# A bank of 512 columns for one token tile: new traversal of the output products in the merge blocks, and joint evictions of token-major pairs, in an encoder layer on one core

## The chip, the cores and the metric

The kernel runs on one core of a Trainium2 chip. The core has TensorE (PE in the profile; its weight loads are listed apart as PEld), VectorE (DVE), ScalarE (ACT), GpSimd (POOL) and SyncE (SP), which here issues nearly all DMAs. The metric is the device time of one execution in microseconds.

## The reference

Two sequences, `x_prompt` of 1024 tokens and `x_sample` of 2048, each with 16 meta tokens ahead of it, go through one encoder layer with shared weights and a model width of 1024. What is computed, cut to what matters here:

```python
xn = _rmsnorm(h, g_pre)
proj = xn @ w_in + b_in.astype(xn.dtype)
na_q, na_k, na_v, na_z, ml_qk, ml_v, ml_z, ml_o, ml_g, mg = jnp.split(proj, SPLIT_IDX, axis=-1)
ya = _neighbourhood_attention(...)
ya = (ya.reshape(B, L, NA_WIDTH) * jax.nn.silu(na_z)) @ w_a
yb = (_mlstm_branch(...) * jax.nn.silu(ml_z)) @ w_b
ga, gb = jnp.split(jax.nn.sigmoid(mg), 2, axis=-1)
y = (ga * ya + gb * yb) @ w_out
return h + _rmsnorm(y, g_post)
```

The change touches two places: the products with `w_out` (with the sum of squares that the last norm needs and the factor `g_post`), and the columns of the first projection that are kept token-major (`na_v`, `ml_v`, `ml_z`, `ml_o` and the gates).

## The kernel before

Everything is fp32 in memory. Each large product is made of three matmuls on parts of the operands that are split into a high and a low half (`whi`, `wlo` for weights; `xh`, `xl` or `mh`, `mlo` for data): high by high, high by low, low by high. TensorE's program order is the order in which the Python program emits it; for ACT, DVE, POOL and SP the compile step orders the instructions itself, by a simulated timeline, except for those that `self.behind` pins in program order. Two generators feed TensorE in turn: `dense` (projections and merges) and `sparse` (mLSTM and neighbourhood attention), each yielding an estimated PE time, so that the products of one are strewn among those of the other.

**Weights** come in units of 128 partitions by 1024 fp32. A unit lies in one of four pairs of buffers (`NBW = 4`, tiles `whi` and `wlo`). `wtake` hands out the next unit; `wdone` says that a unit has been used up, and `wpump` then fills the free pair with the next unit of a fixed list. A unit that is used for the first time is loaded raw (`wraw`, two buffers, line 245), split by ACT (line 271) and DVE (line 272) and written back in two parts (line 287). From its second use on it is loaded as two finished parts of 512 KB (line 264).

**PSUM banks** of 128 by 512 fp32 are named by tag: three for `pj` (projections, merges and output products), two for `tr`, one for `sc`, two for `sm`. The attention uses `tr`, `sc` and `sm` alone.

**Token-major projection**, `tm_unit`: for two weight units (halves of the contraction) and pairs of token tiles, each tile of a pair takes a `pj` bank of its own, 24 matmuls fill 256 (or 264) columns of it (lines 644 to 646), and DVE adds the bias into half `a` of a staging tile `stT` (line 661 for the second sequence, line 659 with a factor for the first). After the second tile `tm_store` sends the pair to memory.

**A merge block**, `final`, handles 512 tokens; there are six of them, two of `x_prompt` and four of `x_sample`. In its first half, the merge, eight column tiles by two branches are multiplied (lines 172 to 174 with `yh`, `yl`, 512 columns each) and gated by DVE (lines 2009 and 2011), and split into `mh` (ACT, 2012) and `mlo` (DVE, 2013). In its second half come the output products: `prods` issues 12 matmuls of 256 columns (lines 2042 to 2044) for one token tile, one weight unit (half of the contraction) and a quarter of the columns. For each quarter `cq` there are two banks, each with a pair of token tiles side by side, and two units; each unit is taken, used for the four token tiles and given back at once. After the second unit `leave` is called for both tiles of a bank: ACT squares 256 columns and sums them into one column of `ssq` (line 2047), then DVE multiplies the same 256 columns by `gpost` into `yo` (line 2048). So a full block has 32 calls of `prods`, eight units and 16 leaves. The last block has this order for two quarters only and then a tail in which the token tiles finish one after the other and go through `final_out` at once.

While the products run, a `hook` prepares the next block: `yload` loads its operands (`yl`, line 1936) and splits them with ACT (line 1956) and DVE (line 1940), one step for each call of `prods`. It starts after the sixth call. The attention's own loads (`qr`, `kr`, `gt`, `zt`, `vr`, lines 1310 to 1334), the gates `tg` (line 1981), residuals `xres` (2103) and stores (`out`, 2125) pass through the same SP queue as the weights.

Of the kernel before, what the change touches and what calls it, by code (L numbers as in the profile page):

```python
# [10 lines left out]
F32 = mybir.dt.float32  # L11
F32R = mybir.dt.float32r
I32 = mybir.dt.int32
AF = mybir.ActivationFunctionType
ALU = mybir.AluOpType
# [3 lines left out]
P = 128  # L19
TCARGS = dict(schedule_with_timeline_sim=True)  # L20
D = 1024
KT = D // P
# [95 lines left out]
def _bc(ap, off, n, parts=P):  # L118

    return bass.AP(tensor=ap.tensor, offset=ap.offset + off, ap=[[0, parts], [1, n]])  # L120

NBW = 4
C512, C256 = 0.235, 0.12
# [3 lines left out]
class K:  # L127
# [491 lines left out]
    def tm_unit(self, col, halves, wd):  # L619
        nc, wp = self.nc, self.wp  # L620
        ws = self.wtake(2)
        bb = wp.tile([P, WU], F32, name="bb", bufs=2)
        nc.sync.dma_start(bb[:, :wd], _bc(self.i["b_in"], col, wd))
        todo = []
        for x, s, t0, meta in halves:
            base = NM if meta else 0
            todo += [(x, s, base + 2 * P * j, P, 2, t0 + 2 * P * j) for j in range(2)]
            if meta and not (C_MZ <= col < C_GA - wd):
                todo.append((x, s, 0, NM, 1, None))
        for j, (x, s, c, n, cnt, tok) in enumerate(todo):  # L630
            st = wp.tile([P, 2, WU], F32, name="stT", bufs=4)
            for a in range(cnt):
                p = self.psum("pj", [P, 512])
                o = p[:n, :wd]
                xs = slice(c + a * P, c + a * P + n)
                for k in range(KT):
                    wh, wl = ws[k // 4][0][:, k % 4, :], ws[k // 4][1][:, k % 4, :]
                    if tok is None:
                        both = [(p[:48, :wd], self.xmm[:, k, :], wh), (o, self.xmm[:, k, :NM], wl)]
                        for y, (out, lhs, rhs) in enumerate(both if k < KT - 1 else both[::-1]):  # L640
                            nc.tensor.matmul(out, lhs, rhs, start=k == y == 0, stop=k == KT - 1 and y == 1, skip_group_check=True)
                    else:
                        xh, xl = x[0][:, k, xs], x[1][:, k, xs]
                        nc.tensor.matmul(o, xh, wh, start=k == 0, stop=False)  # L644
                        nc.tensor.matmul(o, xh, wl, start=False, stop=False)  # L645
                        nc.tensor.matmul(o, xl, wh, start=False, stop=k == KT - 1)  # L646
                    if k == 3:
                        if j == len(todo) - 1 and a == cnt - 1:
                            self.wdone()
                        yield (8 if tok is None else 12) * C256  # L650
                if j == len(todo) - 1 and a == cnt - 1:
                    self.wdone()
                if tok is None:
                    nc.scalar.activation(st[:n, 1, :wd], p[32:48, :wd], AF.Copy)
                    nc.vector.tensor_tensor(st[:n, 0, :wd], p[:n, :wd], st[:n, 1, :wd], op=ALU.add)
                    nc.vector.scalar_tensor_tensor(st[:n, 0, :wd], st[:n, 0, :wd], self.rc[:n, 8:9], bb[:n, :wd], op0=ALU.mult, op1=ALU.add)
                elif s == 0:
                    r = tok // P + a
                    nc.vector.scalar_tensor_tensor(st[:n, a, :wd], p[:n, :wd], self.rc[:n, r:r + 1], bb[:n, :wd], op0=ALU.mult, op1=ALU.add)
                else:  # L660
                    nc.vector.tensor_tensor(st[:n, a, :wd], p[:n, :wd], bb[:n, :wd], op=ALU.add)
                if a == cnt - 1:
                    self.tm_store(col, wd, s, n, cnt, tok, st)
                yield 12 * C256
# [1300 lines left out]
    def final(self, s, b, nxt):  # L1965
        nc, fp, i = self.nc, self.wp, self.i
        n, t0 = 512, 512 * b
# [3 lines left out]
        _, yh, yl = self.y  # L1971
# [18 lines left out]
        for ft, br in order:  # L1990
            if br:
                held[ft] = self.wtake(1)[0], tgs.pop(ft)
            w, ms = held[ft]
# [6 lines left out]
            p = self.psum("pj", [P, 512])  # L2000
# [18 lines left out]
            for _ in self.fout:  # L2019
                pass  # L2020
        yt = [fp.tile([P, D], F32, name="yo", tag="xr", bufs=4) for _ in range(4)]
        ssq = fp.tile([P, 4, 4], F32, name="ssq", bufs=2)
        sqj = fp.tile([P, 256], mybir.dt.bfloat16, name="sqj", tag="thT", bufs=1)
        hook = None
        if self.fresh:
            self.fresh = False
# [11 lines left out]
        def prods(o, tt, w, a, fresh):  # L2038
            xs = slice(tt * P, tt * P + P)
            for k in range(4):  # L2040
                f, q = 4 * a + k, w[0][:, k, :]
                nc.tensor.matmul(o, mh[:, f, xs], q, start=fresh and f == 0, stop=False, skip_group_check=True)  # L2042
                nc.tensor.matmul(o, mh[:, f, xs], w[1][:, k, :], start=False, stop=False, skip_group_check=True)  # L2043
                nc.tensor.matmul(o, ml[:, f, xs], q, start=False, stop=f == KT - 1, skip_group_check=True)  # L2044

        def leave(o, tt, cq):
            nc.scalar.activation(sqj, o, AF.Square, accum_out=ssq[:, tt, cq:cq + 1])
            nc.vector.tensor_tensor(yt[tt][:, cq * 256:(cq + 1) * 256], o, self.gpost[:, cq * 256:(cq + 1) * 256], op=ALU.mult)

        for cq in range(4 if nxt else 2):  # L2050
            banks = [self.psum("pj", [P, 2, 256]) for _ in range(2)]
            for a in range(2):
                w = self.wtake(1)[0]
                for tt in range(4):
                    prods(banks[tt // 2][:, tt % 2], tt, w, a, tt % 2 == 0)
                    if tt == 3:
                        self.wdone()
                    if a and tt % 2:
                        for t in (tt - 1, tt):
                            leave(banks[t // 2][:, t % 2], t, cq)  # L2060
                        if nxt and hook is None:
                            if nxt[0] != "f":
                                nres = []
                                hook = self.build_half(*nxt[:2], nres)
                            else:
                                hook = self.ystart(*nxt[1:])
                    if hook:
                        next(hook, None)
                    yield 12 * C256
        if not nxt:  # L2070
            ws = [[self.wtake(1)[0] for _ in range(2)] for _ in range(2)]
            for tt, cq in [(0, 2), (1, 2), (0, 3), (1, 3), (2, 2), (2, 3), (3, 2), (3, 3)]:
                o = self.psum("pj", [P, 512])[:, :256]
                for a in range(2):
                    prods(o, tt, ws[cq - 2][a], a, True)
                    if a == 0:
                        yield 12 * C256
                leave(o, tt, cq)
                if cq == 3:
                    for _ in self.final_out(s, t0, yt, ssq, tt, tt + 1):  # L2080
                        pass
                yield 12 * C256
            self.wdone(4)
# [183 lines left out]
```

## Time and profile before

| What | us |
|---|---|
| median of 3 runs | 2720.48 (2719.08 to 2722.17) |
| profiled execution, its own time | 2718.74 |
| its span | 2717.0 |
| PE busy in it | 2686.7 |
| DVE busy / ACT busy | 1766.1 / 1520.2 |
| first output product, last output product | begin at 2056.1 and 2708.4 |

The span is the time from the first instruction of the program to the last in the profiled execution. The 1.74 us between its span and its own time are outside any instruction. PE is busy in nearly the whole span; matmuls overlap in the pipeline (a matmul of 256 columns is listed at 0.28 us and the next one starts 0.12 us later), so counts of matmuls and stretches of time tell more than summed durations. The DMA traffic is 657.53 MB, 242 GB/s on average, and nearly all of it goes through SP's one hardware queue.

### The profile page before, as it was taken

To read this page: it belongs to the slowest core of one execution; us is meant where nothing else is said; L and a number is where in the kernel's file an instruction comes from. 1 tells how busy PE (TensorE), PEld (TensorE's weight loads), DVE (VectorE), ACT (ScalarE), POOL (GpSimd) and SP (SyncE) were. 2 spreads that over 40 slices of the span, in tenths; PEclk is the share of its full clock that TensorE was granted. 3 is DMA by queue.
4 is the path that set the end of the run, shared out by engine and by line. 5 is a ranking of instruction groups with operands and counts; after the bars stand their busy time and mean duration, and the time that the engine had idled before them with its cause. 6 is when DMAs were issued, how large, how long until landed. Compare 5 with 4: busy or idle time off the path is not lost.

```text
span 2717.0 us, 47583 instructions
## 1 busy us (share of the span) xinstructions
PE 2686.7 (99%) x16696; PEld 2394.5 (88%) x16696; DVE 1766.1 (65%) x4376; ACT 1520.2 (56%) x3375; POOL 126.0 (5%) x294
## 2 busy tenths in 40 slices
PE   9999999999999999999999999999999999999998
PEld 7999988879998889998878888888879898989988
DVE  5557765535777747775424857574658879687864
ACT  5233354435555656666535757564648686767641
POOL 0005000005000013000000000000000000000000
PEclk9999999999999999999999999999999999999999
DMA  9984454369865797757486666786599999898955
GB/s 369 340 283 143 138 187 158 102 239 343 265 222 174 264 325 227 229 175 234 144 294 191 222 202 209 262 278 201 163 299 332 313 298 295 245 317 244 324 208 220
DMA packets 351507, 657.53 MB, mean 242 GB/s; under 512 B 53444, under 2 KB 158868, under 8 KB 351268
## 3 DMA queue, kind: packets, MB, share of 16 engines
q1 hardware_dynamic: 344004, 645.46, 71.7%
q0 software_dynamic: 7264, 9.04, 1.2%
q8 instruction: 131, 2.15, 0.3%
q14 instruction: 108, 0.88, 0.1%
HBM read 438.64 MB, written 215.66 MB: 241 GB/s over the span
## 4 chain that ended last, share of the span: by engine, by line
PE 88%; DMA 7%; DVE 2%; ACT 2%; issue 1%; SPq 1%; POOL 0%; DVEq 0%; ACTq 0%; POOLq 0%
PE pj L172 14%; PE pj L173 14%; PE pj L174 14%; PE pj L644 5%; PE pj L645 5%; PE pj L646 5%; PE sm L1407 3%; PE pj L2042 2%; PE pj L2044 2%; PE pj L2043 2%; PE tr L1393 2%; PE sm L174 2%; PE sm L173 2%; PE sm L172 2%; DMA wraw<-wu 1%; DMA wlo<-wl 1%
## 5 line engine op out<-in xcount | busy, mean ns | idle before, releaser
L172 PE MATMUL pj<-xh,whi 128*128 128x512 f32 (+1 forms) x1480 | 580.2, 392 | 4.6 <-ACT st L569 3.6
L173 PE MATMUL pj<-xl,whi 128*128 128x512 f32 (+1 forms) x1480 | 565.8, 382 | 0.2 <-DVE xl L345 0.2
L174 PE MATMUL pj<-xh,wlo 128*128 128x512 f32 (+1 forms) x1480 | 565.1, 382 | 0.3 <-DVE wlo L272 0.3
L644 PE MATMUL pj<-whi,xh 128*128 128x256 f32 (+1 forms) x1152 | 330.9, 287 | 0.0
L174 PEld LDWEIGHTS pj<-xh,wlo 128*128 128x128 f32 x1480 | 278.2, 188 | 58.2 <-DVE wlo L272 0.6
L172 PEld LDWEIGHTS pj<-xh,whi 128*128 128x128 f32 x1480 | 278.5, 188 | 54.1 <-ACT st L569 4.4
L645 PE MATMUL pj<-wlo,xh 128*128 128x256 f32 (+1 forms) x1152 | 325.0, 282 | 0.6 <-DMA wlo<-wl 0.6
L646 PE MATMUL pj<-whi,xl 128*128 128x256 f32 (+1 forms) x1152 | 324.8, 282 | 0.0
L173 PEld LDWEIGHTS pj<-xl,whi 128*128 128x128 f32 x1480 | 278.8, 188 | 46.2 <-issue 0.7
L2042 PE MATMUL pj<-whi,mh 128*128 128x256 f32 x768 | 220.3, 287 | 0.0
L645 PEld LDWEIGHTS pj<-wlo,xh 128*128 128x128 f32 x1152 | 217.1, 188 | 0.9 <-DMA wlo<-wl 0.8
L644 PEld LDWEIGHTS pj<-whi,xh 128*128 128x128 f32 x1152 | 217.3, 189 | 0.4
L646 PEld LDWEIGHTS pj<-whi,xl 128*128 128x128 f32 x1152 | 217.0, 188 | 0.0
L2043 PE MATMUL pj<-wlo,mh 128*128 128x256 f32 x768 | 217.0, 283 | 0.0
L2044 PE MATMUL pj<-whi,mlo 128*128 128x256 f32 x768 | 216.9, 282 | 0.0
L1396 DVE TENSOR_TENSOR pts<-tr,pts 96x384 fp32r<-96x384 f32 (+2 forms) x192 | 118.5, 617 | 64.7 <-ACT pts L1395 63.8
L172 PE MATMUL pj<-yh,whi 128*128 128x512 f32 x384 | 154.2, 401 | 1.8 <-DVE tg L2009 1.1
L173 PE MATMUL pj<-yl,whi 128*128 128x512 f32 x384 | 151.0, 393 | 0.2 <-DVE yl L1420 0.2
L174 PE MATMUL pj<-yh,wlo 128*128 128x512 f32 x384 | 151.0, 393 | 0.0
L2043 PEld LDWEIGHTS pj<-wlo,mh 128*128 128x128 f32 x768 | 146.1, 190 | 1.0
L2042 PEld LDWEIGHTS pj<-whi,mh 128*128 128x128 f32 x768 | 146.0, 190 | 1.0
L2044 PEld LDWEIGHTS pj<-whi,mlo 128*128 128x128 f32 x768 | 145.9, 190 | 0.0
(459 smaller groups left out, 6171.7 us busy)
## 6 DMA issues: line engine op xcount, KB each, us to landing
whi<-wh SPq DMA_DIRECT2D x140, 512.0 KB
wlo<-wl SPq DMA_DIRECT2D x140, 512.0 KB
wraw<-wu SPq DMA_DIRECT2D x64, 512.0 KB
wh<-whi SPq DMA_DIRECT2D x64, 512.0 KB
wl<-wlo SPq DMA_DIRECT2D x64, 512.0 KB
gt<-st SPq DMA_DIRECT2D x96, 256.0 KB
tg<-gt SPq DMA_DIRECT2D x96, 256.0 KB
xt<-xt SPq DMA_DIRECT2D x32, 512.0 KB
```

Source lines behind the costliest of these rows:

```text
L172: mm(out, ah, bh, start=start, stop=False, **more)
L173: mm(out, ah, bl, start=False, stop=False, **more)
L174: mm(out, al, bh, start=False, stop=stop, **more)
L644: nc.tensor.matmul(o, xh, wh, start=k == 0, stop=False)
L645: nc.tensor.matmul(o, xh, wl, start=False, stop=False)
L646: nc.tensor.matmul(o, xl, wh, start=False, stop=k == KT - 1)
L1393: nc.tensor.transpose(pt[:ks, ch, :], pr_[:, ch * ks:(ch + 1) * ks], self.ident)
L1396: nc.vector.tensor_tensor(pts[:ks, :nb, 1, :], pt[:ks, :nb], pts[:ks, :nb, 0, :].bitcast(F32), op=ALU.subtract)
L1407: nc.tensor.matmul(av[:, cb % 2], vt[:ks, kc // 8 + ch].rearrange("p a b -> p (a b)"), pts[:ks, ch].rearrange("p a b -> p (a b)"), start=c ...
L2042: nc.tensor.matmul(o, mh[:, f, xs], q, start=fresh and f == 0, stop=False, skip_group_check=True)
L2043: nc.tensor.matmul(o, mh[:, f, xs], w[1][:, k, :], start=False, stop=False, skip_group_check=True)
L2044: nc.tensor.matmul(o, ml[:, f, xs], q, start=False, stop=f == KT - 1, skip_group_check=True)
```

## The change

In `tm_unit`, for the second sequence and widths up to 256, the two tiles of a pair share one bank, the first in columns 0 to 255 and the second in 256 to 511. Only the pair's very first matmul carries the start flag. DVE evicts both in one instruction of 2 by 256 columns, with the bias broadcast over the two. The 264 columns wide units, the first sequence and the meta tokens stay as they are.

In `final`, a bank now holds 512 columns of one token tile. For each half of the columns (`cp`) there are two passes, one for each pair of token tiles. The first pass takes four weight units one after the other and keeps them, the second pass uses the same four and gives each back after its second product. Each pass has two banks and eight calls of `prods` (four units by two tiles); the two banks are left after the last unit, each with one square of 512 columns and one multiplication of 512 columns. `ssq` has two columns in use for each token tile (three in the last block) in place of four. The hook starts after the fifth call. The last block does this for one half of the columns, and its tail is as before, save for the column of `ssq`.

```diff
             st = wp.tile([P, 2, WU], F32, name="stT", bufs=4)
+            pair = s and tok is not None and 2 * wd <= 512
             for a in range(cnt):
-                p = self.psum("pj", [P, 512])
-                o = p[:n, :wd]
+                if not pair or not a:
+                    p = self.psum("pj", [P, 512])
+                o = p[:n, wd * a:wd * a + wd] if pair else p[:n, :wd]
...
-                        nc.tensor.matmul(o, xh, wh, start=k == 0, stop=False)
...
+                        nc.tensor.matmul(o, xh, wh, start=k == 0 and not (pair and a), stop=False, skip_group_check=True)
...
-                else:
+                elif not pair:
                     nc.vector.tensor_tensor(st[:n, a, :wd], p[:n, :wd], bb[:n, :wd], op=ALU.add)
+                elif a:
+                    two = bb[:, :wd].rearrange("p (t c) -> p t c", t=1).to_broadcast([P, 2, wd])
+                    nc.vector.tensor_tensor(st[:, :, :wd], p[:, :2 * wd].rearrange("p (t c) -> p t c", t=2), two, op=ALU.add)
...
-        ssq = fp.tile([P, 4, 4], F32, name="ssq", bufs=2)
-        sqj = fp.tile([P, 256], mybir.dt.bfloat16, name="sqj", tag="thT", bufs=1)
+        ssq = fp.tile([P, 4, 3], F32, name="ssq", bufs=2)[:, :, :2 if nxt else 3]
+        sqj = fp.tile([P, 512], mybir.dt.bfloat16, name="sqj", tag="thT", bufs=1)
...
-        def leave(o, tt, cq):
-            nc.scalar.activation(sqj, o, AF.Square, accum_out=ssq[:, tt, cq:cq + 1])
-            nc.vector.tensor_tensor(yt[tt][:, cq * 256:(cq + 1) * 256], o, self.gpost[:, cq * 256:(cq + 1) * 256], op=ALU.mult)
-
-        for cq in range(4 if nxt else 2):
-            banks = [self.psum("pj", [P, 2, 256]) for _ in range(2)]
-            for a in range(2):
-                w = self.wtake(1)[0]
-                for tt in range(4):
-                    prods(banks[tt // 2][:, tt % 2], tt, w, a, tt % 2 == 0)
-                    if tt == 3:
-                        self.wdone()
-                    if a and tt % 2:
-                        for t in (tt - 1, tt):
-                            leave(banks[t // 2][:, t % 2], t, cq)
-                        if nxt and hook is None:
+        def leave(o, tt, c0, n, q):
+            nc.scalar.activation(sqj[:, :n], o, AF.Square, accum_out=ssq[:, tt, q:q + 1])
+            nc.vector.tensor_tensor(yt[tt][:, c0:c0 + n], o, self.gpost[:, c0:c0 + n], op=ALU.mult)
+
+        for cp in range(2 if nxt else 1):
+            ws = []
+            for pair in range(2):
+                banks = [self.psum("pj", [P, 512]) for _ in range(2)]
+                for u in range(4):
+                    if not pair:
+                        ws.append(self.wtake(1)[0])
+                    for t in range(2):
+                        tt, o = 2 * pair + t, 256 * (u // 2)
+                        prods(banks[t][:, o:o + 256], tt, ws[u], u % 2, u == 0)
+                        if pair and t:
+                            self.wdone()
+                        if u == 3:
+                            leave(banks[t], tt, 512 * cp, 512, cp)
+                        if nxt and hook is None and u == 2:
...
-                leave(o, tt, cq)
+                leave(o, tt, 256 * cq, 256, cq - 1)
```

More of the change, by code (lines that the diff above doesn't have):

```diff
@@ L643, in tm_unit @@
                         xh, xl = x[0][:, k, xs], x[1][:, k, xs]
-                        nc.tensor.matmul(o, xh, wh, start=k == 0, stop=False)
-                        nc.tensor.matmul(o, xh, wl, start=False, stop=False)
-                        nc.tensor.matmul(o, xl, wh, start=False, stop=k == KT - 1)
+                        nc.tensor.matmul(o, xh, wh, start=k == 0 and not (pair and a), stop=False, skip_group_check=True)
+                        nc.tensor.matmul(o, xh, wl, start=False, stop=False, skip_group_check=True)
+                        nc.tensor.matmul(o, xl, wh, start=False, stop=k == KT - 1, skip_group_check=True)
                     if k == 3:
@@ L2066, in final @@
                                 hook = self.ystart(*nxt[1:])
-                    if hook:
-                        next(hook, None)
-                    yield 12 * C256
+                        if hook:
+                            next(hook, None)
+                        yield 12 * C256
         if not nxt:
```

## The prediction

> **What bounds the kernel now.** I read the page first: busy shares, then the table of PE's waits, then busy time by stretches for the output products. Of the page this line counts:
>
> ```profile
> PE 2686.7 (99%) x16696; PEld 2394.5 (88%) x16696; DVE 1766.1 (65%) x4376; ACT 1520.2 (56%) x3375; POOL 126.0 (5%) x294
> ```
>
> The change leaves the number and the shape of the matmuls alone: 32 calls of 12 matmuls of 256 columns in a full block, before and after, and 48 matmuls for a token-major pair. So PE's 2686.7 us stay, and the time can move only by what PE idles, some 30 us of a span of 2717.0. Where does it idle? The stretches of the six runs of output products, one row each (the columns: length, then busy us with instruction counts for PE, PEld, DVE, ACT, POOL, then granted clock, DMA share, GB/s):
>
> ```profile
> 2056.00:2118.00 62.00, 61.02 (x508) 60.73 (x507) 49.81 (x114) 51.51 (x125) 0.00 (x0) 1.00 1.00 338
> 2177.00:2241.00 64.00, 62.82 (x510) 61.76 (x508) 45.62 (x107) 51.81 (x120) 0.00 (x0) 1.00 0.94 298
> 2303.00:2371.00 68.00, 64.41 (x512) 63.32 (x510) 44.21 (x105) 49.39 (x117) 0.00 (x0) 0.97 0.85 251
> 2431.00:2493.00 62.00, 62.00 (x509) 61.37 (x509) 44.90 (x106) 47.33 (x116) 1.03 (x2) 1.00 0.93 275
> 2552.50:2615.00 62.50, 62.16 (x510) 61.46 (x509) 41.82 (x104) 43.97 (x113) 0.00 (x0) 1.00 0.74 241
> 2662.50:2709.00 46.50, 46.22 (x386) 45.94 (x385) 17.73 (x64) 7.93 (x32) 0.00 (x0) 1.00 0.48 182
> ```
>
> PE's idle time here is 0.98 + 1.18 + 3.59 + 0 + 0.34 + 0.28 = 6.4 us, and the DMA engines are 0.74 to 1.00 busy while ACT is 0.70 to 0.83 busy in the five full blocks. What ended PE's waits from 2000 us on, and in the token-major stage (last row, of the whole span):
>
> ```profile
> PE sm L1407 <- ACT prb L1376: 6.1, 4, 3.6
> PE sm L1407 <- DVE yg L1414: 1.4, 2, 1.2
> PE pj L172 <- DVE tg L2009: 1.1, 1, 1.1
> PE pj L645 <- DMA wlo<-wl: 0.6, 1, 0.6
> ```
>
> Nothing waits for a `leave`, for a bank of the output products or for their weights. The waits are those of the attention (`sm`) for ACT. In the token-major products the only wait is 0.6 us for a weight, which the change does not touch.
>
> The longest wait, 3.59 us in the third block, is worth following, since it shows who is late. The chain of waits (start, length), ACT's and PE's timeline and the clock:
>
> ```profile
> 2322.97 9.66 DMA kr<-nkm
> ...
> 2332.72 1.06 ACT L1344 ACTIVATE kd<-kr 64x1024 fp32r<-64x1024 f32 x1 [3.47 <-DMA kr<-nkm]
> 2334.35 0.36 ACT L2047 ACTIVATE sqj<-pj 128x256 bf16<-128x256 f32 x1
> 2337.94 0.38 ACT L2047 ACTIVATE sqj<-pj 128x256 bf16<-128x256 f32 x1
> 2339.55 1.01 PE L1407 MATMUL sm<-pts,vt 128*128 128x256 f32 x3 [3.59 <-ACT prb L1376]
> ...
> 2340.00:2342.50 2.50, 2.50 (x14) 2.50 (x14) 2.23 (x5) 2.50 (x6) 0.00 (x0) 0.50 1.04 226
> ```
>
> A load of the attention took 9.66 us in a full DMA queue, ACT stood for it 3.47 us in its program order, two squares queued behind it, and PE starved. Afterwards the clock was 0.50 for a slice of 2.5 us: 1.25 us more. The first cause is DMA traffic, not ACT's load.
>
> **The change part by part.** *Evictions.* Their groups (line, engine, op, tiles, shape, count | busy us, mean ns), and two operations of 512 columns out of PSUM to price the new ones:
>
> ```profile
> L2047 ACT ACTIVATE sqj<-pj 128x256 bf16<-128x256 f32 x96 | 36.4, 379 | 48.5 <-PE pj L2044 43.9 <-DVE yo L2048 3.9
> L2047 ACT ACTIVATION_READ_ACCUMULATOR sqj<-pj 128x1 f32 x96 | 18.9, 197 | 0.0
> L2048 DVE TENSOR_TENSOR yo<-pj,gain 128x256 f32<-128x256 f32 x96 | 40.3, 419 | 38.7 <-ACT sqj L2047 38.1
> L661 DVE TENSOR_TENSOR stT<-pj,bb 128x256 f32<-128x256 f32 x96 | 40.3, 420 | 27.9 <-PE pj L646 26.2 <-DMA nv<-stT 0.6
> L569 ACT ACTIVATE st<-pj,bfm 128x512 f32<-128x512 f32 x59 | 40.0, 682 | 61.4 <-PE pj L174 49.2 <-DVE pj L557 8.1 <-issue 4.0
> L1395 ACT ACTIVATE pts<-tr 128x512 fp32r<-128x512 f32 x32 | 19.0, 594 | 8.7 <-PE tr L1393 8.4
> L2009 DVE SCALAR_TENSOR_TENSOR tg<-tg,pj 128x512 f32<-128x512 f32 x96 | 65.4, 682 | 18.7 <-PE pj L174 17.4
> ```
>
> A full block has 8 leaves in place of 16. A square of 512 columns is not in the trace: 0.594 to 0.682 us by these rows; I take 0.62, without a bias as the copy at 0.594. ACT: 16 x (0.379 + 0.197) = 9.2 us become 8 x (0.62 + 0.197) = 6.5, so 2.7 us less. DVE: 16 x 0.419 = 6.7 become 8 x 0.682 = 5.5, so 1.2 less. The last block, where four leaves replace eight, saves half of that. The token-major stage replaces 96 x 0.420 by 48 x 0.682, 7.6 us of DVE less in all. All this lies beside PE's matmuls. It is worth 0 where PE doesn't wait; the most it can give is the idle time that ACT and DVE cause in these stretches. I credit 2 us of the 6.4 (bounds: 0, and the 6.4 plus 1.25 of slow clock), since the 3.59 us came from a load. The token-major pair counts 0: its one eviction ends 0.26 us later after the second half, with two whole banks of 48 matmuls ahead before that bank is needed.
>
> *The turn of the banks.* Before, a bank complete at one call came up for new matmuls four calls later, with two squares and two multiplications in between. Now the first bank of a pass is needed two calls later (between: the last product of its sister and the first of the next pass). A call's time follows from line 2042, which has four matmuls in each:
>
> ```profile
> 2431.00:2493.00 62.00, 36.71 (x128) 24.25 (x128) 1.00 0.93 275
> 2662.50:2709.00 46.50, 36.09 (x128) 24.30 (x128) 1.00 0.48 182
> ```
>
> 128 / 4 = 32 calls: 62 / 32 = 1.94 us with the attention's matmuls strewn in, 46.5 / 32 = 1.45 us in the last block without them. The allowance is thus 3.9 us, or 2.9. A leave that starts at once needs 0.62 + 0.197 + 0.682 = 1.5 us; it fits if ACT and DVE start no more than 2.4 us late together. After the late load above the squares were 3.6 us apart, so in such a moment it doesn't fit, but then PE starves already. I take 0, bounds 0 and 0.9 us at each turn (rival 3).
>
> *Weights held through two passes.* This is the part with a price. Before, a unit was given back every four calls, and its successor in the buffer was needed 12 calls later: 23 us. Now the units of a half are held through the first pass and given back every second call of the second, and each successor is needed six calls later: 11.6 us (8.7 in the last block, 7.2 for two of its units). Also the third and fourth unit of a block are needed at its fifth and seventh call in place of the ninth and 13th, with the buffer of the fourth free only at the end of the merge: 11.6 us again. What does a refill take? From issue to landing, transfers of the chain in the output stretches:
>
> ```profile
> 2301.30 5.77 DMA wlo<-wl
> 2307.09 10.03 DMA vr<-nv
> ...
> 2565.08 5.49 DMA tg<-gt
> ```
>
> So 5.5 to 10 us, and before it the wait for the place in SP's queue. SP's timeline and its main wait show that:
>
> ```profile
> 2433.19 0.33 SPq L264 DMA_DIRECT2D whi<-wh  x1
> 2434.96 0.32 SPq L264 DMA_DIRECT2D wlo<-wl  x1
> ...
> 2437.36 4.21 SPq L1936 DMA_DIRECT2D yl<-yb  x4
> 2441.61 1.35 SPq L1936 DMA_DIRECT2D yl<-ya  x2
> 2443.99 1.97 SPq L1981 DMA_DIRECT2D tg<-gt  x3
> 2446.32 0.32 SPq L264 DMA_DIRECT2D wlo<-wl  x1
> 2446.97 0.32 SPq L264 DMA_DIRECT2D whi<-wh  x1
> ...
> SPq L264 <- PE pj L2044: 85.1, 24, 7.2
> ```
>
> The fourth unit, free at about 2431.5, had its second part issued at 2434.96: 3.5 us later. The next, free four calls on at 2439.2, went out at 2446.97, 7.8 us later, behind `yl` and `tg`. Today's 23 us hide that. With 11.6 us, 3.5 + 10 = 13.5 is 1.9 us late; a refill issued at once, its parts 0.65 us apart as at 2446.32 and 2446.97, takes 0.65 + 5.8 = 6.4 and isn't late. In favour: the hook starts a call earlier, inside the first pass, in which no weight is given back, so `yl` has the queue to itself and the refills come after it. Against: in the second pass four units, 4 MB, fall into 15.5 us, 270 GB/s beside the attention's loads, where the whole stretch moves 241 to 338. SP stands for a buffer already (24 times, up to 7.2 us); it will stand at other moments, with `qr`, `kr`, `gt`, `zt` and `vr` queued behind, and PE's attention matmuls wait for those. I take one short wait of 1 us in each of five blocks: 5 us. Bounds: 0, and rival 2.
>
> The rest counts nothing: the reduction over two or three columns is a single small DVE operation, and nothing changes behind the last product, where PE has nothing left.
>
> **Sum.** 0 for the matmuls, -2 for the relief, +5 for weights: +3 us on the profiled 2718.74, whose span is 2717.0. That execution lies 1.7 us under the median of 2720.48, so I add the 3 us to the median: 2723. What a measurement of this kernel can tell from no change is about 0.2%, 5.4 us: below 2715 is faster, above 2726 slower.
>
> **Rivals.** *1, relief wins.* If the shorter ACT and DVE work and a DMA queue freed in the first pass remove all the 6.4 us and the 1.25 us of slow clock, the time is 2713. For it: every wait in these stretches ends at ACT or DVE. Against: the largest begins with a load. *2, weights late (slower).* The place is the second pass of each half and the start of a block; it decides from 11.6 us between giving back and landing. At 7.8 + 10 us a unit is 6.2 us late, and then the slow clock adds 1.25. One such wait in two of ten halves, and 1.5 us in the other eight, make 15 + 12 = 27 us: 2747; one of 1.9 us in each half less the relief makes +17: 2737, which I take for this case. For it: DMA shares of 0.93 to 1.00 and 7.8 us behind `yl`. Against: a refill today is issued that late because nothing presses it. The Trainium skill, "TensorE: Matmul & The Clock Gate", Part 1, says that about 3.4 us of idling bring the array to half clock. The trace agrees with 3.59 us idle and 0.50 after it; by this rule the short waits of my sum cost only themselves. *3, the banks' turn binds.* There are 3 x 5 + 1 = 16 turns. If ACT takes the square 3.3 us late at each, a turn costs 3.3 + 1.5 - 3.9 = 0.9 us: 14 us, 2734; at half of them 7 us, 2727, which I take. For it: ACT 0.83 busy in the first two blocks. Against: no wait for a leave today.
>
> **How the numbers follow.** Forecast (within 0.2%) 0.52, rival 1 0.14, rival 2 0.25, rival 3 0.09. So faster 0.14, same 0.52, slower 0.34. The forecast's own range is 2716 to 2727. The range for all reaches from 2712, just under rival 1, to 2740, above rivals 2 and 3; the dear end of rival 2 at 2747 is left out.
>
> **What would show it.** Right: PE busy within a few us of 2686.7; 52 squares in all, 44 of them of 512 columns at about 0.62 us; ACT busy down by about 15 us and DVE by about 14; waits of PE at the output products for `whi`, `wlo` of one or two us each. Wrong: waits of the output products for the multiplication by `gpost` (rival 3), several weight waits above 3 us with slices of 0.50 clock (rival 2), or idle time in the six stretches near 0 (rival 1). What would break the reasoning altogether: PE's busy time itself changing by more than 5 us, or the compile step ordering SP's queue so differently that merges or mLSTM, untouched here, gain or lose waits.

## The result and the profile after

| | before | changed |
|---|---|---|
| median of 20 runs each, us | 2718.80 | 2725.02 |
| ratio (95% interval) | | 1.0021 (1.0013 to 1.0029) |
| span of the profiled execution, us | 2717.0 | 2727.7 |

The change costs 0.21%, some 6 us. The forecast was 2723, three more than the 2720.48 measured until then; the sign and the mechanism came out, and the size is at the edge of what was called no change. The profiled execution of the changed kernel took 2729.48 us, 4.5 us more than the median of its runs: single executions scatter by as much as the effect.

The page of the changed kernel, the line that answers to the first one quoted of before:

```profile
PE 2692.0 (99%) x16696; PEld 2397.9 (88%) x16696; DVE 1759.3 (64%) x4284; ACT 1514.2 (56%) x3287; POOL 125.3 (5%) x294
```

The matmuls are the same in number, and yet PE's busy time is 5.3 us more. That is no extra work: three stretches of 3.41 us ran at half clock ahead of the last product (at 213, 2108 and 2449 us), where before there was one (at 2340 us), and a matmul at half clock counts as busy for longer (0.41 us at 2449.2 where 0.28 is usual). Two stretches more make 3.4 of the 5.3 us; the trace does not name the rest. The evictions came out as priced (groups of the changed kernel: count, busy us, mean ns):

```profile
L2052 ACT ACTIVATE sqj<-pj 128x512 bf16<-128x512 f32 x44 | 26.1, 594 | 28.4 <-PE pj L2049 27.8
L2052 ACT ACTIVATION_READ_ACCUMULATOR sqj<-pj 128x1 f32 x52 | 10.2, 195 | 0.0
L666 DVE TENSOR_TENSOR stT<-pj,bb 128x512 f32<-128x512 f32 x48 | 32.9, 685 | 12.6 <-PE pj L648 11.7 <-DMA nv<-stT 0.5
L2053 DVE TENSOR_TENSOR yo<-pj,gain 128x512 f32<-128x512 f32 x44 | 30.3, 689 | 36.1 <-ACT sqj L2052 35.9
```

What PE waited for from 2000 us on, in the changed kernel:

```profile
PE sm L1412 <- ACT prb L1381: 3.7, 3, 1.5
PE pj L2048 <- DMA wlo<-wl: 2.6, 2, 1.7
PE pj L2047 <- DMA whi<-wh: 1.6, 2, 1.4
PE pj L2048 <- DVE wlo L272: 1.4, 1, 1.4
PE pj L2049 <- DVE mlo L2018: 1.2, 2, 0.6
PE pj L172 <- DVE tg L2014: 0.8, 1, 0.8
```

Beside the table of before, these lines give the main terms. The attention's wait for ACT fell from 6.1 to 3.7 us. Four lines are new, all at the output products (2047 to 2049), and all for an operand: 5.6 us for a weight (a DMA, or in the first block the split of a raw unit) and 1.2 us for `mlo`. No line waits for the multiplication by `gpost`, so the quicker turn of the banks costs nothing.

One of these waits followed through, at the start of the fourth block. The last matmul that reads the third unit before its refill, in PE's timeline of the changed kernel:

```profile
2434.33 0.39 PE L174 MATMUL pj<-yh,wlo 128*128 128x512 f32 x1
```

SP's timeline behind it (start, us of issuing):

```profile
2433.48 1.88 SPq L2133 DMA_DIRECT2D out<-yo  x2
2435.41 0.43 SPq L2111 DMA_DIRECT2D xres<-x_sample  x1
2437.51 0.45 SPq L1330 DMA_DIRECT2D qr<-nq  x1
2438.52 0.33 SPq L264 DMA_DIRECT2D whi<-wh  x1
2439.78 0.32 SPq L264 DMA_DIRECT2D wlo<-wl  x1
```

And the transfer, in the chain of waits, and the matmul that waited for it, in PE's timeline:

```profile
2439.78 9.04 DMA wlo<-wl
...
2448.86 0.39 PE L2048 MATMUL pj<-wlo,mh 128*128 128x256 f32 x1 [1.70 <-DMA wlo<-wl]
```

And SP's own waits between 2434 and 2440 us:

```profile
SPq L1330 <- DMA vr<-nv: 1.6, 1, 1.6
SPq L264 <- DMA wlo<-wl: 0.9, 1, 0.9
SPq L264 <- DMA whi<-wh: 0.5, 1, 0.5
```

The buffer of the block's third unit was read for the last time at 2434.7. SP had two stores, a residual and a load of the attention ahead of the refill, and stood for 3.0 us until earlier transfers had landed; it issued the two parts 3.8 and 5.1 us after the last reader. The second took 9.0 us to land, 14.1 us in all, of which 12 went to transfers under way, its own and earlier ones. The unit is needed at the fifth call of the block; before the change it was the ninth. The wait is 1.70 us, and the price goes on (stretches behind it: length, PE, PEld, DVE, ACT, POOL, clock, DMA share, GB/s):

```profile
2449.00:2452.60 3.60, 3.60 (x18) 3.60 (x19) 0.08 (x1) 0.61 (x2) 0.00 (x0) 0.53 1.02 382
2452.60:2456.00 3.40, 3.40 (x28) 3.30 (x28) 2.42 (x5) 3.03 (x5) 0.00 (x0) 1.00 1.05 383
```

18 matmuls start in 3.6 us, 28 in the 3.4 us that follow. A clock of 0.53 over 3.6 us loses 0.47 x 3.6, another 1.7 us.

Where did the profile's own +10.7 us come from? The first product of the first merge block starts here in the two kernels, and the last output product here (the one of before at 2708.20):

```profile
2003.56 0.40 PE L172 MATMUL pj<-yh,whi 128*128 128x512 f32 x1
```

```profile
2008.22 0.40 PE L172 MATMUL pj<-yh,whi 128*128 128x512 f32 x1
2718.94 0.28 PE L2047 MATMUL pj<-whi,mh 128*128 128x256 f32 x1
```

The merge stage takes 704.6 us before and 710.7 changed, 6.1 more. The other 4.7 us lie ahead of it; the same start is at 2006.0 in a second profile of the changed kernel, and between 2002.1 and 2009.0 in those of the experiments, so this part may well be scatter; no run isolates it. (1.7 of it is the stretch of half clock at 213 us, which the second profile of the changed kernel and that of run 10 have too.) Of the 6.1 us, 2.9 are waits of PE (13.1 against 10.2 us from 2000 us on) and 1.7 a second stretch of half clock. The trace does not name the other 1.5 us.

### The profile page after: what moved, and what is told of

Its sections match the earlier page's. It is cut to its first block, busy times and chain, and to the rows that moved or that the text cites. A ratio compares the mean times of both kernels' runs of the same rounds, so it can differ in the third digit from the quotient of the medians.

```text
span 2727.7 us, 47381 instructions
## 1 busy us (share of the span) xinstructions
PE 2692.0 (99%) x16696; PEld 2397.9 (88%) x16696; DVE 1759.3 (64%) x4284; ACT 1514.2 (56%) x3287; POOL 125.3 (5%) x294
## 4 chain that ended last, share of the span: by engine, by line
PE 85%; DMA 9%; DVE 3%; ACT 2%; issue 1%; SPq 0%; POOL 0%; DVEq 0%; ACTq 0%; POOLq 0%
PE pj L172 13%; PE pj L173 13%; PE pj L174 13%; PE pj L646 5%; PE pj L647 5%; PE pj L648 5%; PE pj L2049 3%; PE pj L2048 3%; PE pj L2047 3%; PE sm L1412 2%; PE tr L1398 2%; PE sm L174 2%; PE sm L173 2%; PE sm L172 2%; DMA wlo<-wl 1%; DMA kr<-nk 1%
```

## Experiments

Theory H: the loss comes from the output products, where units held through two passes leave the refills half as many calls. Theory T: the token-major evictions cost. Further rivals stand in the expectations. All runs are timed in five rounds beside the kernel before.

**1. The token-major part alone** (the products as before).

> Only the token-major part of the change (joint eviction of a pair), the output products as before. Theory H (the loss comes from the output products: units held through two passes leave refills six calls instead of twelve, and the last column tile of the merge is needed two calls earlier): no difference, ratio 0.999 to 1.001, and no PE wait for a weight at the output products. Theory T (the joint eviction costs, as the 1.47 us wait for the attention's yg at 1021 us in the changed profile may hint): the whole loss of about 6 us is here, ratio 1.002.

Measured: ratio 0.9996 (0.9987 to 1.0005). PE has no wait for a weight at the output products. The 1.47 us wait at 1021 us is 0.6 us here. Theory T falls.

**2. The output products' part alone.**

> Only the output products' part of the change, token-major as before. Theory H: the whole loss, ratio 1.002 (about +6 us), with PE waits of 4 to 7 us in all at the output products for whi, wlo and mlo. Theory T: ratio 1.000, and the waits at the output products cost nothing because other waits go.

Measured: ratio 1.0035 (1.0022 to 1.0048), with these waits:

```profile
PE pj L2042 <- DMA whi<-wh: 2.7, 2, 2.3
PE pj L2043 <- DMA wlo<-wl: 1.9, 2, 1.7
PE pj L2043 <- DVE wlo L272: 1.4, 1, 1.4
PE pj L2044 <- DVE mlo L2013: 1.2, 2, 0.6
```

7.2 us of waits for operands, just over what was expected. The whole loss is here, and nothing of it in run 1.

**3. Another order of the four units.**

```diff
-                        tt, o = 2 * pair + t, 256 * (u // 2)
-                        prods(banks[t][:, o:o + 256], tt, ws[u], u % 2, u == 0)
+                        tt, o = 2 * pair + t, 256 * (u % 2)
+                        prods(banks[t][:, o:o + 256], tt, ws[u], u // 2, u == 0)
```

(with the list of units, and the last block's tail, in the same order)

> The whole change, but the four units of a half are used in another order: the first contraction half for both column quarters, then the second. So mh and mlo of column tiles 4 to 7 are needed at the fifth call of a block, as before the change, and not at the third. Theory H: the two waits for mlo (0.61 and 0.59 us) are gone, the waits for whi and wlo stay: 1 to 2 us below the changed kernel, ratio to before 1.0015 to 1.002. Rival (the mlo waits are only a place where PE stands anyway, and a weight is late right after): no difference to the changed kernel, the waits reappear at whi or wlo.

Measured: ratio 1.0031 (1.0019 to 1.0043). The waits for `mlo` are gone, and those for weights are 8.5 us (2.9 + 2.4 for loads, 1.9 + 1.3 for the split) against 5.6 in the changed kernel. So the rival holds: PE that doesn't stand for `mlo` stands for a weight.

**4. Two leaves for each bank.**

```diff
-                            leave(banks[t], tt, 512 * cp, 512, cp)
+                            for q in range(2):
+                                leave(banks[t][:, 256 * q:256 * q + 256], tt, 512 * cp + 256 * q, 256, 2 * cp + q)
```

> The whole change, but each bank of 512 columns is left in two halves of 256, each with its own square and multiplication, as many instructions as before the change. It takes away the relief of ACT (2.7 us a block) and DVE and keeps the held units. If the relief was worth the 2 us that the prediction credits: 2 us slower than the changed kernel, with more PE wait for ACT at the attention. If relief is worth nothing (ACT waits come from late loads): equal to the changed kernel within 1 us. If the banks' turn binds: PE waits for the multiplication by gpost appear, several us.

Measured: ratio 1.0038 (1.0026 to 1.0050), above the changed kernel's, with intervals that just touch. Its profile:

```profile
PE pj L2048 <- DMA wlo<-wl: 4.1, 3, 3.0
PE pj L2048 <- DVE wlo L272: 3.6, 2, 2.0
PE sm L1412 <- ACT prb L1381: 2.5, 4, 1.2
PE pj L2047 <- DVE yo L2053: 2.0, 3, 1.3
```

Now the banks' turn binds: 2.0 us for `yo`, a wait that is in no other profile here. So the larger leave is what keeps the quicker turn free. The waits for weights are 9.3 us as well, against 5.6, so the turn alone does not explain the time. The attention's wait for ACT is 2.5 us, not more than in the changed kernel, though ACT has its 16 leaves a block back: the fall from 6.1 us is not due to fewer evictions.

**5. Giving back two calls later.**

```diff
-                        if pair and t:
-                            self.wdone()
+                        if pair and t and u:
+                            self.wdone(1 + u // 3)
```

> The changed kernel, but each of the first three units of a half is given back two calls later, so that its refill has four calls (7.8 us) and not six (11.6 us). Nothing else changes. Theory H (late refills make the loss): the PE waits for whi and wlo grow from 5.6 us to 12 to 20 us, with more stretches of half clock, and the stage from the first merge product to the last output product grows from 710.7 us in the changed kernel to 720 to 730; ratio to before 1.006 to 1.009. Rival (the refills are ahead anyway and the waits at the output products are only the place where PE catches up with other late loads): within 2 us of the changed kernel.

Measured: ratio 1.0015 (1.0005 to 1.0025), within the interval of the changed kernel. This was no test of theory H. PE's timeline in the third block, and then SP's, show why:

```profile
2329.30 0.28 PE L2049 MATMUL pj<-whi,mlo 128*128 128x256 f32 x1
```

```profile
2329.50 0.33 SPq L264 DMA_DIRECT2D wlo<-wl  x1
2329.91 0.38 SPq L264 DMA_DIRECT2D whi<-wh  x1
```

The matmul of 2329.30 ends the tenth call and is the last that reads the first unit of the half, and the refill goes out with it, two calls before the program gives the unit back. `wdone` only places the load in the program; the wait is for the last reader. To shorten a refill's time, the reader must move (run 9).

**6. The first half's units used again**, in blocks two to five.

```diff
-            ws = []
+            same = nxt and (s, b) != (0, 0)
+            ws = ws if cp and same else []
...
-                    if not pair:
+                    if not pair and not (cp and same):
```

(the units left out of the list, and nothing given back in these blocks' first halves)

> The changed kernel, but in blocks two to five the second half of the output columns is multiplied with the units of the first half, which are kept: the last four units of these blocks are neither loaded nor given back in between. Left out: the products with the second half of w_out in these blocks. No refill can be late there but at the third and fourth unit of a block. Theory H: of the waits for whi and wlo those in the middle of blocks two to five go (1.6 us in the changed kernel's trace), those at the start of a block (2.6 us) and in the first block (1.4 us) stay; 2 to 5 us below the changed kernel, ratio to before 1.000 to 1.002. If the loss has nothing to do with the refills: as the changed kernel.

Measured: ratio 1.0014 (1.0004 to 1.0024). In the middle of blocks two to five no wait for a weight is left. At the start of the third block it is 5.1 us (1.6 + 3.5), in the first block 1.4. That is as theory H has it, in one profile; the gain on the changed kernel (1.0021) is within the intervals.

**7. The new order only in second halves.** The first two quarters and the last block run the loop of before.

> Only the second half of the columns takes the new order; the first two quarters, and the last block, take the old one (units given back at once, banks of two token tiles), token-major as in the change. Then only the last unit of a block has its refill cut to six calls (the one before to eight, then ten), the third and fourth unit of a block are needed as late as before, and mlo too. Theory H: waits for whi, wlo and mlo at the output products below 1 us in all, half of the relief stays; ratio to before 0.998 to 1.000. Rival (the passes themselves or the shifted hook cost): half of the loss stays, ratio 1.001 to 1.002.

Measured: ratio 1.0017 (1.0007 to 1.0026): the rival's value, not the expected one. The profile says where:

```profile
PE sm L1412 <- ACT prb L1381: 4.2, 2, 3.0
PE pj L2047 <- ACT whi L271: 2.1, 1, 2.1
PE pj L2048 <- DVE wlo L272: 1.1, 1, 1.1
```

The two weight waits are for units being split by ACT and DVE, which happens in the first block only; outside it 0.3 us are left. The attention's 3.0 us wait for ACT in the third block is back with the old first half.

**8. The changed kernel again.**

> The changed kernel once more, unaltered, beside the next three on the same chip. It tells how far its waits in the profile and its time scatter. Every theory: ratio to before 1.001 to 1.003; if the places of its waits for whi and wlo in the profile move by several us, single waits of one profile are no measure.

Measured: ratio 1.0022 (1.0010 to 1.0033). The sum of waits for weights is 6.0 us against 5.6, but the largest (3.2 us) is at 2326, at the start of the third block, which has none in the first profile. So the sums of the two profiles agree, and their places don't. One place holds over the experiments, though: of the ten profiles in which the third block has the new first half, nine show waits of 1.5 to 5.1 us at its seventh call (runs 2 to 6, 8 to 10 and 12). That call is the first to need the fourth unit, whose buffer comes free only at the end of the merge. The first profile of the changed kernel is the tenth, and no profile with the old first half has the wait.

**9. Second pass by token tiles.**

```diff
-                for u in range(4):
+                for u, t in [(x // 2, x % 2) if not pair else (x % 4, x // 4) for x in range(8)]:
```

> The changed kernel with the second pass of each half in another order: all four units for the third token tile, then all four for the fourth. A unit is now last read at the 13th to 16th call of its half and no longer at the tenth, 12th, 14th and 16th, so its refill has three, four, five or six calls (5.8, 7.8, 9.7, 11.6 us). The bank of the third tile is left four calls earlier, which relieves the banks' turn. Theory H (refills): by the landings in the changed kernel's trace (5 to 14 us after the last use) about half of the refills are late by 1 to 6 us: waits for whi and wlo of 15 to 30 us in all, ratio to before 1.006 to 1.012. Rival (banks' turn or anything but the refills): equal to the changed kernel or faster, ratio 1.000 to 1.002.

Measured: ratio 1.0047 (1.0031 to 1.0063), against 1.0022 in the same session. Its profile:

```profile
PE pj L2047 <- DMA whi<-wh: 4.0, 4, 2.0
PE pj L2048 <- DMA wlo<-wl: 3.9, 3, 2.4
PE pj L2047 <- ACT whi L271: 2.2, 1, 2.2
PE pj L172 <- DMA whi<-wh: 1.3, 1, 1.3
```

With two more lines of 1.0 (split) and 0.4 us, weights are waited for 12.8 us, more than twice as long as in the changed kernel, and now in merges too (line 172). The dose works, and the relieved banks' turn brings nothing. Waits and ratio are less than was expected (15 to 30 us, 1.006 to 1.012); that one late refill gives the next ones time would explain it, but is not shown.

**10. The first block in the old order.**

> The changed kernel, but the first block keeps the old order (there each unit is loaded raw, split and written back, with the DMA engines at 1.00). Theory H with the first block as its main place (waits of 1.3 to 3.2 us for the split units and a stretch or two of half clock in every profile): ratio to before 1.0005 to 1.0015, no waits at the first block's output products. If the other blocks' refills make the loss: as the changed kernel, 1.002.

Measured: ratio 1.0015 (1.0004 to 1.0025), beside 1.0022 (1.0010 to 1.0033) for the changed kernel in the same session: a difference well within the intervals. No wait for split units; 3.0 us for loads and 0.6 for `mlo` in the other blocks.

**11. The new order in second halves of blocks two to five only.**

> The new order only for the second half of the columns and only in blocks two to five; the first block, the last and all first halves keep the old one, token-major joint as in the change. Theory H: no unit is needed earlier than before at a block's start, none waits to be split, and only one refill in a block has six calls: no wait for weights at the output products above 0.5 us, ratio to before 0.998 to 1.000. If the passes cost by something else than refills: ratio 1.001 or more, as with the second halves of all blocks.

Measured: ratio 1.0000 (0.9989 to 1.0010), as expected, with one wait for a weight of 1.0 us where none above 0.5 was expected. Against run 7 only the first block differs.

**12. The new order in first halves of blocks two to five only.**

> The complement of the run before: the new order only for the first half of the columns in blocks two to five, the old one for the second halves, the first block and the last. Here the third and fourth unit of a block are needed at its fifth and seventh call, mlo of the last column tile at its third, and one refill in a block has six calls (the next ones eight, ten and twelve). Theory H with the start of a block as the main place outside the first block: waits for whi, wlo and mlo of 2 to 4 us in all at the starts of blocks, nearly all of what is left of the loss when the first block keeps the old order: ratio to before 1.001 to 1.002. If the loss outside the first block came from the refills between the halves and not from the start: ratio 1.000.

Measured: ratio 1.0001 (0.9992 to 1.0010), against the expectation. The wait at a block's start is there, but the one for ACT is shorter for it:

```profile
PE sm L1412 <- ACT prb L1381: 2.8, 2, 1.5
PE pj L2050 <- DMA wlo<-wl: 2.1, 1, 2.1
```

What is lost at the weight in this profile, 2.1 us, is about what the attention gains (6.1 before, 2.8 here), and each of the two profiles has one stretch of half clock in this stage, behind the 2.1 us here and behind the 3.59 us before. So the start of a block comes out as a draw. No version here beats the kernel before.

## Why the prediction was right

**Matmuls, 0.** Right: 16696 before and after. That PE's busy time moves by 5 us was named as what would break the reasoning; it did move, by 5.3, with the same work: 3.4 of it is the clock's, and the rest is not explained.

**Evictions.** The durations of ACT's squares were to fall by 15 us and fell from 55.3 to 39.4 (26.1 + 10.2, and 3.1 for the eight of 256 columns); DVE's were to fall by 14 and did. The prediction worded this sign as busy time of the engines, and there it failed: by the page ACT's fell only by 6.0 us (1520.2 to 1514.2) and DVE's by 6.8 (1766.1 to 1759.3). The two are different measures: all of ACT's groups add up to 1676.5 us before, where the page has 1520.2, so durations that overlap count once there. A square of 512 columns takes 0.594 us, the lower bound, and not 0.62.

**Relief, -2 us.** The wait for ACT fell by 2.4 us (6.1 to 3.7), near the forecast, and not for the reason of the sum; that is luck. With as many evictions as before (run 4) the wait for ACT is as short; with the old first half (runs 7 and 11) the 3.0 us wait in the third block is back. It goes with the order of the first half. The traces show how. SP's timeline in the third block, before and then changed:

```profile
2320.31 0.45 SPq L1325 DMA_DIRECT2D qr<-nq  x1
2320.99 0.40 SPq L264 DMA_DIRECT2D whi<-wh  x1
2321.61 0.32 SPq L264 DMA_DIRECT2D wlo<-wl  x1
2322.32 0.45 SPq L1326 DMA_DIRECT2D kr<-nk  x1
2322.97 0.45 SPq L1327 DMA_DIRECT2D kr<-nkm  x1
```

```profile
2327.09 1.10 SPq L1330 DMA_DIRECT2D qr<-nq  x1
2328.28 0.55 SPq L1331 DMA_DIRECT2D kr<-nk  x1
2329.12 0.44 SPq L1332 DMA_DIRECT2D kr<-nkm  x1
2332.56 0.33 SPq L264 DMA_DIRECT2D wlo<-wl  x1
```

Before, a refill of two parts goes out between `qr` and `kr`. The new first pass gives no unit back, so `kr` follows at once and the next refill comes 3.4 us behind it. ACT's `kd`, which the prediction found waiting 3.47 us for `kr`, waits for no load here (it starts at 2340.32). It is the same in every profile read for it: with the old first half (before, runs 1, 7 and 11) a refill lies between and `kd` waits 2.9 to 3.5 us, with the new one (changed, runs 3, 4, 8, 10 and 12) neither. That a quieter queue helps stands in the prediction, but under the first rival ("a DMA queue freed in the first pass") and not in the sum.

**Banks' turn, 0.** Right in the changed kernel; run 4 shows that the margin is small.

**Weights, +5 us.** Right in place and nature: refills with six calls, those of a half's second pass (PE waits for them in the next half's first pass) and those at the start of a block, short waits of 0.2 to 1.7 us (up to 3.2 in the second profile), 5.6 and 6.0 us in all. Runs 2, 9 and 11 bear it out: present with the passes, doubled where readers move back, down to 1.0 us at 1.0000 where no unit is both raw and held and no block start is pressed. Where it was mis-sized: the prediction let short waits cost only themselves. Two of the places, 1.41 us after 0.97 and 1.70 alone, were each followed by 3.41 us of half clock, 1.7 us more apiece, against one such stretch before. Where it did price the slow clock, it took 1.25 us from one slice of 2.5 us; that stretch too lasted 3.41 us and cost 1.7. And five blocks with 1 us each is not how it falls: the fifth has no wait for a weight in either profile of the changed kernel, and in the first block the split of a raw unit is what is late, which the prediction priced at nothing of its own. Run 11 against run 7 puts 0.17% there, with intervals that nearly part (0.9989 to 1.0010, 1.0007 to 1.0026); run 10 against run 8, in one session, puts 0.07% there, with intervals that overlap widely. So the first block's share is not settled.

**A step that was missed.** The last column tile's `mlo` is needed two calls earlier, since the second contraction half comes at the third call and no longer at the fifth. It shows as 1.2 us; run 3, which has no such wait, is no faster (1.0031), so no loss can be put down to it.

**Sum.** +3 forecast, about +6 measured. In the two main profiles the terms came out larger than the sum had them, on both sides: 5.6 us of waits for weights, 3.4 of half clock behind them and 1.2 for `mlo`; against that, 2.4 us less wait for ACT, 1.2 less for `yg` and 1.7 of half clock that no longer follows the 3.59 us. So +10.2 and -5.3 stand for +5 and -2, and the errors partly cancel: that the sum is nearer than its terms is luck. So is part of the forecast time: 2723 is 2 us off 2725.02, while the change of 6.2 us is missed by 3, since the 2720.48 of three runs lay 1.7 us above the median of 20. The rivals that the relief wins, and that the banks' turn binds, are out. The rival of late weights had the right mechanism, at a price of 17 us nearly three times the measured one.

What stays open: blocks two to five lose nothing with one new half, the first or the second, but with both, and the last block's, the ratio is 1.0015 (run 10). Its interval doesn't exclude that the parts add up to it. Run 12 loses nothing in spite of its 2.1 us at a weight, so a sum of waits for weights does not give the time by itself. The hook's start, a call earlier, was not tried alone.

## What to carry to other kernels

Holding operands through a second pass halves the time that their refills have, even though the bytes stay the same; so count calls from the last reader to the next first reader, and compare that with issue delay plus landing from the trace (here 11.6 us against 14.1 in the refill followed above), before saving evictions on engines that are rarely waited for. A buffer comes free with its last reader and not where the program says so: to test a refill's slack, move the reader. On an engine that is 99% busy an operand that is 1.7 us late may cost 3.4.

## What the hardware showed

The granted clock fell to half after single idle times of PE of 1.7 to 3.6 us, and also after two shorter ones within some 4 us: 0.97 and 1.41 us in the changed kernel (ending at 2103.7 and 2106.4), 0.72 and 0.90 us in run 9 (at 2193.1 and 2194.4). Ahead of the last product each slow stretch lasted 3.41 us or twice that. The shortest single one is the 1.70 us before 2448.86 shown above. It isn't a threshold: in run 11 a wait of 1.84 us for `yg` ended at 2209.4 and the next stretch kept the full clock (PE's timeline, then the stretch):

```profile
2209.42 0.59 PE L1412 MATMUL sm<-pts,vt 128*128 128x256 f32 x3 [1.84 <-DVE yg L1419]
...
2209.40:2213.00 3.60, 3.58 (x29) 3.60 (x30) 1.95 (x6) 3.13 (x9) 0.00 (x0) 1.00 1.06 219
```

The Trainium skill ("TensorE: Matmul & The Clock Gate", Part 1) names an idle window of about 3.4 us and says that the window runs free of the kernel. The length of the slow stretches agrees; the shortest single idle time that one followed was half as long here.
